# Gathered value rows summed in four column strips instead of two, with seven gather buffers

## The chip, the cores and the metric

The kernel runs on one core of a Trainium2 chip. The metric is the device time of one execution in microseconds (us); runs of the kernel before took 4088.43 to 4096.79 us. Five engines work in parallel, each through its own queue in order: PE (TensorE, matmuls), DVE (VectorE), ACT (ScalarE), POOL (GpSimd, which issues the gathers here) and SP (which issues most other transfers). They wait for each other and for transfers through semaphores.

## The reference, cut to what matters

One layer of a streaming encoder for 1152 tokens (1024 of a prompt, 8 x 16 of running streams) of width 1024: RMS norm, a gated convolution beside an RWKV-7 time mixing, then a retrieval over 16384 single-neuron experts. Only the retrieval's last step is touched by the change:

```python
def block(xt):                                   # 128 tokens
    q = (xt @ wq).reshape(PEER_BLOCK, PEER_HEADS, 2, PEER_HALF)
    ...
    eidx = jnp.take_along_axis(cidx, pos, axis=-1)          # 8 heads x 16 experts a token
    gate = jax.nn.softmax(sc, axis=-1)
    u = jnp.take(U, eidx, axis=0)
    act = jax.nn.gelu(jnp.einsum('thkd,td->thk', u, xt).astype(jnp.float32))
    coef = (gate * act).astype(xt.dtype)
    return jnp.einsum('thk,thkd->td', coef, jnp.take(V, eidx, axis=0))
```

So each token takes 128 rows of U and 128 rows of V, 1024 floats each.

## The kernel before, in words

The nine tiles of 128 tokens go through the time mixing in three groups (`GROUPS`, `base(g)`). The retrieval has two ways. Four tiles (`DENSE`) multiply with all experts (`dense()`): first the gate matrices are made from one-hot products and written to memory (`gates_of`, with `hidden_ahead` beside it), then for each block of 128 experts `hidden` makes the activations (matmuls into `ph`) and `out_half` adds up the outputs (matmuls into `po`). The other five tiles are sparse: they gather only the rows that they need.

- `sparse_u` (L1009) takes a tile's 128 picks k one by one: one indirect DMA, issued by POOL at L1028, fetches the row of U of pick k for all 128 tokens (512 KB into a buffer `gt`), and one DVE instruction multiplies it with the token's input and sums it into column k of `hu`.
- `sparse_v` (L1036) does the same with V, but sums on PE. The coefficients are first transposed, so that partition and pick change places; a gather (L1075) then fetches for one token its 128 rows of V, and a matmul with contraction 128 sums them. The stationary operand is a slice of `cex` of 128 x 32 that is zero but for one column, so the token's sum falls in one of 32 output rows and 32 tokens add up in the same 32 partitions of `pv` (named `sv` in the profile). There are four such column strips of 32. `summed` issues four fp32 matmuls for two tokens, one of strip 2hc+1 and one of strip 2hc for each half of the 1024 columns:

```python
for hf in range(2):
    for c in (1, 0):
        q = 32 * (2 * hc + c)
        mm = P.matmul(pv[q:q + 32, hf * 512:(hf + 1) * 512], cex[:, lo:lo + 32], ...
```

The buffers `gt` are a ring of `NGT` = 6, shared by rows of U, rows of V and a few others; a gather waits until the buffer of the gather six places earlier has been read. `side()` steps through one `sparse_v` and one `sparse_u` at a time, two steps each in turn; a step is one gather. `run` weaves these steps into the main work: before the dense part one step per 900 ns of PE work (`PACE_B`; 1500 ns where only one of the two is there), in it so that they spread evenly over what is left (`until`). PE's queue is in order: a matmul of `sv` whose row has not landed holds up the main work behind it.

The slots `sl` (`NSL` = 27, in `slot()`) hold the time mixing's intermediate tiles. In the first group some gate tiles use `gt` buffers as `room`, since no gather runs then. `hidden` loads one block of `u_t` (512 KB, `ur`), and ACT and DVE split it into two parts for PE.

Of the kernel before, what the change touches and what calls it, by code (L numbers as in the profile page):

```python
# [9 lines left out]
F32 = mybir.dt.float32  # L10
# [20 lines left out]
NPT = 8  # L31
NSL = 27
LAT = 350
SPREAD = (16, 8)
PACE_B = (900, 1500)
EARLY = 40e3
NGT, NGD = 6, 0
AWAY = [4, 5, 6, 7]
# [58 lines left out]
def body(ctx, tc, A):  # L97
# [87 lines left out]
    def f32(ap):  # L185
        return ap.bitcast(F32)
# [130 lines left out]
    def base(g):  # L317
# [18 lines left out]
        if smp:  # L336
            ss = T(bp, [128, KB, 8], F32, "shst", 1)
            nc.sync.dma_start(ss, A["state_shift"])
            S.activation(xh[:, :, n:n + 8], ss, AF.Copy)
            V.tensor_tensor(xl[:, :, n:n + 8], ss, f32(xh[:, :, n:n + 8]), op=OP.subtract)  # L340
# [571 lines left out]
    def route(row, vals, idxs):  # L912
# [62 lines left out]
        yield 6 if row == 0 else 2 * SPREAD[until[0] is not None]  # L975
        gate = T(sp, [128, 8, 16], F32, "gate_d", 1) if row in DENSE else T(sp, [128, 8, 16], F32, "gate", 3)
        V.tensor_tensor(gate, sc, sc[:, :, 0:1].to_broadcast([128, 8, 16]), op=OP.subtract)
# [24 lines left out]

    more = [None, 0]

    def gathered():
# [7 lines left out]
    def sparse_u(row, ei, et, gate):  # L1013
# [12 lines left out]
        for k in range(128):  # L1026
            ug = gathered()
            G.indirect_dma_start(out=ug, out_offset=None, in_=A["peer_u"],  # L1028
                                 in_offset=bass.IndirectOffsetOnAxis(ap=ei[:, k:k + 1], axis=0))
            if due:  # L1030
                dot(*due)
            due = k, ug
            yield
        dot(*due)
        sparse_v_q.append((row, hu, et, gate))

    def sparse_v(row, hu, et, gate):
# [6 lines left out]

        cw = cex[:, :1024].rearrange("p (two c t w) -> p two c t w", two=2, c=2, w=32)
        c4 = ct_.rearrange("p (c b t) -> p c b t", c=4, t=8)

        def fill(n):
            if n < 8:
                V.tensor_copy(cw[:, n % 2, :, :, 31], c4[:, 2 * (n // 4):2 * (n // 4) + 2, n % 4])  # L1050

        def summed(hc, i, vgs):

            prev = mains[1]
            for hf in range(2):
                for c in (1, 0):
                    lo = 32 * (16 * (i // 8 % 2) + 8 * c + i % 8) + 31 - i
                    q = 32 * (2 * hc + c)
                    mm = P.matmul(pv[q:q + 32, hf * 512:(hf + 1) * 512], cex[:, lo:lo + 32],
                                  vgs[c][:, hf * 512:(hf + 1) * 512], start=i == 0, stop=i == 31, side=True)  # L1060
                    behind(mm, prev)
                    prev = mm
            if i % 8 == 0:
                fill(4 * hc + i // 8 + 1)

        fill(0)
        due = None
        for hc, i in ((a, b) for a in range(2) for b in range(32)):
            vgs = []
            for c in range(2):  # L1070
                if c and due:
                    summed(*due)
                t = 64 * hc + 32 * c + i
                vg = gathered()
                G.indirect_dma_start(out=vg, out_offset=None, in_=A["peer_v"],  # L1075
                                     in_offset=bass.IndirectOffsetOnAxis(ap=et[:, t:t + 1], axis=0))
                vgs.append(vg)
                yield
            due = hc, i, vgs
        summed(*due)  # L1080
        live[0] -= 1
# [15 lines left out]
    def dense():  # L1097
# [54 lines left out]
        def hidden(k, g):  # L1152

            raw = T(dp, [128, D], F32, "ur", 2)
            nc.sync.dma_start(raw, A["u_t"][k])
            h = T(dp, [128, D], F32R, "uh", 2)
            S.activation(h, raw, AF.Copy)
            lo = T(dp, [128, D], F32R, "ul", 2)
            V.tensor_tensor(lo, raw, f32(h), op=OP.subtract)
            ps = T(pd, [128, ND], F32, "ph", 2)  # L1160
# [93 lines left out]
    def side():  # L1254

        while True:
# [4 lines left out]
            while two[0] or two[1]:  # L1261
                for i in (0, 0, 1, 1):
                    if two[i] and next(two[i], "end") == "end":
                        two[i] = None
                    elif two[i]:
                        steps[0] += 1
                        yield two.count(None)
# [133 lines left out]
```

## Time and profile before

| | us |
|---|---|
| median of 3 runs (lowest, highest) | 4094.19 (4088.43, 4096.79) |
| the profiled execution, its time | 4107.61 |
| its span, first to last instruction | 4105.8 |
| PE busy, share of the span | 3698.5, 90% |
| DVE, POOL, ACT busy | 2765.4, 1631.3, 1476.1 |
| transfer engines, mean busy share | 75% (queues 47.0, 19.8, 7.9, 0.3) |

The time is read by stages: up to about 1000 us the time mixing with gathers of U only from 580 us on; 1000 to 2200 us the rest of the time mixing, with both kinds of gathers; 2200 to 2600 us the gate matrices; from 2800 to 4050 us the dense products. A busy share says little by itself; what matters in each stage is which engine never waits.

### The profile page before, as it was taken

Reading aid. Unit: us, or ns where it says so; the run is one execution under the profiler, and the core shown is the slowest. Engines: PE = TensorE matmul, PEld = TensorE weight load, DVE = VectorE, ACT = ScalarE, POOL = GpSimd, SP = SyncE. Lnnn points to the kernel's source line nnn. Section 1 sums busy time; section 2 is a strip of 40 time slices with the busy share of each in tenths; the row PEclk is TensorE's granted clock in tenths of the full one; section 3 lists DMA queues with packets and bytes.
Section 4 is the critical chain, followed back from the end, with each engine's and each line's share of the span. In section 5 each row is a group of like instructions: output and inputs, shape, how many; then the busy total and the mean of one; then the engine's idle time right before and its main releaser. Section 6 shows DMA issues by size and latency. Waiting matters only on the chain. (4 is left out here: it accounts for less than half of the span.)

```text
span 4105.8 us, 56088 instructions
## 1 busy us (share of the span) xinstructions
PE 3698.5 (90%) x18870; PEld 2666.7 (65%) x18870; DVE 2765.4 (67%) x7426; ACT 1476.1 (36%) x3383; POOL 1631.3 (40%) x1553
## 2 busy tenths in 40 slices
PE   7999977878897878898869999699999999999998
PEld 6777866666475545455635666488766677766666
DVE  5655799887698786576886555699866666543334
ACT  5455533434332323223235567532322222222222
POOL 0000024434556554555565544455444444333320
PEclk9999988988998988898989999899999999999999
DMA  3223436657998888889888877899999888887774
GB/s 100 74 67 95 159 125 227 224 171 254 342 326 285 319 285 277 284 322 329 306 313 307 312 280 255 306 359 338 333 331 328 282 300 290 292 284 263 251 240 143
DMA packets 415584, 1065.20 MB, mean 259 GB/s; under 512 B 44993, under 2 KB 124993, under 8 KB 413249
## 3 DMA queue, kind: packets, MB, share of 16 engines
q0 software_dynamic: 184464, 671.55, 47.0%
q1 hardware_dynamic: 182880, 271.03, 19.8%
q10 hardware_dynamic: 47952, 119.03, 7.9%
q8 instruction: 150, 2.46, 0.2%
q14 instruction: 138, 1.12, 0.1%
HBM read 1000.55 MB, written 61.28 MB: 259 GB/s over the span
## 5 line engine op out<-in xcount | busy, mean ns | idle before, releaser
L1028 POOL DMA_INDIRECT gt<-peer_u,ei x640 | 786.8, 1229 | 1132.8 <-PE sv L142 467.3
L1075 POOL DMA_INDIRECT gt<-peer_v,et x640 | 679.6, 1062 | 652.9 <-PE sv L142 417.3
L142 PE MATMUL mm<-xT,wh 128*128 128x384 f32 (+1 forms) x2880 | 885.1, 366 | 14.1 <-ACT wh L246 12.9
L159 DVE SCALAR_TENSOR_TENSOR gt<-gt,xn 128x1024 f32<-128x1024 f32 x640 | 772.9, 1220 | 181.3 <-DMA gt<-peer_u,ei 122.6
L142 PE MATMUL sv<-gt,c 128*32 128x512 f32 x2560 | 648.9, 634 | 94.7 <-DMA gt<-peer_v,et 94.6
L142 PE MATMUL po<-vh,ph 128*128 128x512 f32 x2048 | 652.7, 392 | 0.0
L142 PEld LDWEIGHTS mm<-xT,wh 128*128 128x128 f32 x2880 | 554.7, 197 | 91.9 <-issue 45.4
L142 PE MATMUL mm<-xT,wl 128*128 128x384 f32 (+1 forms) x1440 | 509.5, 354 | 42.1 <-DVE wl L159 36.4
L142 PEld LDWEIGHTS po<-vh,ph 128*128 128x128 f32 x2048 | 383.2, 188 | 105.1 <-issue 23.5
L142 PE MATMUL ph<-xth,uh 128*128 128x512 f32 x1024 | 412.6, 403 | 31.9 <-ACT ge L1168 31.9
L142 PE MATMUL ph<-xth,ul 128*128 128x512 f32 x1024 | 405.9, 396 | 0.0
L142 PE MATMUL ph<-xtl,uh 128*128 128x512 f32 x1024 | 404.5, 395 | 0.0
L142 PEld LDWEIGHTS sv<-gt,c 128*32 128x32 f32 x2560 | 126.7, 113 | 423.7 <-issue 299.3
L142 PE MATMUL po<-vl,ph 128*128 128x512 f32 x1024 | 401.2, 392 | 0.0
L246 ACT ACTIVATE wh<-raw 128x512 fp32r<-128x512 f32 x432 | 268.6, 628 | 352.0 <-PE mm L142 196.8
L159 DVE TENSOR_TENSOR wl<-raw,wh 128x512 fp32r<-128x512 f32 x432 | 295.1, 686 | 99.5 <-ACT wh L246 85.4
L142 PEld LDWEIGHTS mm<-xT,wl 128*128 128x128 f32 x1440 | 285.2, 198 | 71.4 <-DVE wl L159 47.3
L1195 ACT ACTIVATE vh<-vr 128x512 fp32r<-128x512 f32 x256 | 159.7, 627 | 370.2 <-PE po L142 265.6
L159 DVE TENSOR_TENSOR ge<-ge,cc 128x512 f32<-128x512 f32 x128 | 87.8, 689 | 298.9 <-ACT ge L1168 262.7
L159 DVE TENSOR_SCALAR o<-iota,dt 128x128 f32<-128x128 f32 x640 | 177.4, 347 | 146.8 <-PE po L142 146.4
L1168 ACT ACTIVATE ge<-ph 128x512 f32<-128x512 f32 x128 | 76.4, 598 | 554.6 <-PE ph L142 545.9
L142 PEld LDWEIGHTS ph<-xth,uh 128*128 128x128 f32 x1024 | 193.1, 189 | 116.6 <-issue 41.9
(247 smaller groups left out, 5287.1 us busy)
## 6 DMA issues: line engine op xcount, KB each, us to landing
ur<-u_t SPq DMA_DIRECT2D x128, 512.0 KB
vr<-peer_v ACTq DMA_DIRECT2D x256, 256.0 KB
raw<-w_in SPq DMA_DIRECT2D x240, 256.0 KB
c<-ct ACTq DMA_DIRECT2D x16, 2048.0 KB
cc<-c SPq DMA_DIRECT2D x32, 1024.0 KB
raw<-peer_wq SPq DMA_DIRECT2D x96, 256.0 KB
raw<-w_pab SPq DMA_DIRECT2D x48, 256.0 KB
raw<-w_o SPq DMA_DIRECT2D x48, 256.0 KB
```

The source lines that it names most:

```text
L142: ins = nc.tensor.matmul(out, lhsT, rhs, **kw)
L159: self.last = getattr(nc.vector, name)(*a, **kw)
L246: S.activation(h, part, AF.Copy)
L1028: G.indirect_dma_start(out=ug, out_offset=None, in_=A["peer_u"], in_offset=bass.IndirectOffsetOnAxis(ap=ei[:, k:k + 1], axis=0))
L1075: G.indirect_dma_start(out=vg, out_offset=None, in_=A["peer_v"], in_offset=bass.IndirectOffsetOnAxis(ap=et[:, t:t + 1], axis=0))
L1168: S.activation(g, ps, AF.Gelu_apprx_tanh)
L1195: S.activation(h, raw, AF.Copy)
```

## The change

`sparse_v` now takes four tokens at a time, one of each strip, and issues eight matmuls for them in the order of strips 3, 2, 1, 0 for each half. The sum of four tokens is issued after the third gather of U that follows them when both kinds run (`both`), else after two more gathers of V. `side()` takes four gathers of V, then four of U. The ring `gt` has seven buffers. To make room for it: `NSL` falls to 25, two small tiles share others' buffers (`shst`, `gate_d`), and `hidden` loads `u_t` in two halves of 128 x 512, each split by its own ACT and DVE instruction.

```diff
-NSL = 27
+NSL = 25
...
-NGT, NGD = 6, 0
+NGT, NGD = 7, 0
...
-            ss = T(bp, [128, KB, 8], F32, "shst", 1)
+            ss = T(bp, [128, KB, 8], F32, "bc", 3)
...
-        gate = T(sp, [128, 8, 16], F32, "gate_d", 1) if row in DENSE else T(sp, [128, 8, 16], F32, "gate", 3)
+        gate = T(sp, [128, 8, 16], F32, "d1", 1) if row in DENSE else T(sp, [128, 8, 16], F32, "gate", 3)
...
-        cw = cex[:, :1024].rearrange("p (two c t w) -> p two c t w", two=2, c=2, w=32)
-        c4 = ct_.rearrange("p (c b t) -> p c b t", c=4, t=8)
+        cw = cex[:, :1024].rearrange("p (two c t w) -> p two c t w", two=2, c=4, w=32)
+        c4 = ct_.rearrange("p (c b t) -> p c b t", c=4, t=4)
...
-                for c in (1, 0):
-                    lo = 32 * (16 * (i // 8 % 2) + 8 * c + i % 8) + 31 - i
-                    q = 32 * (2 * hc + c)
+                for c in (3, 2, 1, 0):
+                    lo = 32 * (16 * (i // 4 % 2) + 4 * c + i % 4) + 31 - i
+                    q = 32 * c
...
-        for hc, i in ((a, b) for a in range(2) for b in range(32)):
+        for i in range(32):
             vgs = []
-            for c in range(2):
-                if c and due:
+            for c in range(4):
+                if c == 2 and due:
                     summed(*due)
-                t = 64 * hc + 32 * c + i
+                    due = None
+                t = 32 * c + i
                 vg = gathered()
                 G.indirect_dma_start(out=vg, out_offset=None, in_=A["peer_v"],
                                      in_offset=bass.IndirectOffsetOnAxis(ap=et[:, t:t + 1], axis=0))
                 vgs.append(vg)
-                yield
-            due = hc, i, vgs
-        summed(*due)
+                yield True
+            due = i, vgs
+            yield False
+            if both[0]:
+                summed(*due)
+                due = None
+                yield False
...
-            raw = T(dp, [128, D], F32, "ur", 2)
-            nc.sync.dma_start(raw, A["u_t"][k])
             h = T(dp, [128, D], F32R, "uh", 2)
-            S.activation(h, raw, AF.Copy)
             lo = T(dp, [128, D], F32R, "ul", 2)
-            V.tensor_tensor(lo, raw, f32(h), op=OP.subtract)
+            for c in range(2):
+                cs = slice(512 * c, 512 * c + 512)
+                raw = T(dp, [128, 512], F32, "ur", 2)
+                nc.sync.dma_start(raw, A["u_t"][k][:, cs])
+                S.activation(h[:, cs], raw, AF.Copy)
+                V.tensor_tensor(lo[:, cs], raw, f32(h[:, cs]), op=OP.subtract)
...
-                for i in (0, 0, 1, 1):
-                    if two[i] and next(two[i], "end") == "end":
+                for i in (0, 0, 0, 0, 0, 1, 1, 1, 0, 1):
+                    both[0] = two[1] is not None
+                    if two[i] is None:
+                        continue
+                    got = next(two[i], None)
+                    if got is None:
                         two[i] = None
-                    elif two[i]:
+                    elif got:
                         steps[0] += 1
                         yield two.count(None)
```

PE's queue in the gate stage, kernel before; `sv` is the strip accumulator, `gt` a gathered row, `c` the coefficients. Two sums follow each other with other matmuls between them:

```order
L142 MATMUL sv_4405_19284<-gt_4856_20946,c_17_108 32x512 [waits DMASW6_49]
L142 MATMUL sv_4405_19284<-gt_4850_20918,c_17_108 32x512 [waits DMASW5_49]
L142 MATMUL sv_4405_19284<-gt_4856_20946,c_17_108 32x512
L142 MATMUL sv_4405_19284<-gt_4850_20918,c_17_108 32x512
...
L142 MATMUL sv_4405_19284<-gt_4879_21034,c_17_108 32x512 [waits DMASW0_49]
L142 MATMUL sv_4405_19284<-gt_4878_21011,c_17_108 32x512 [waits DMASW7_49]
L142 MATMUL sv_4405_19284<-gt_4879_21034,c_17_108 32x512
L142 MATMUL sv_4405_19284<-gt_4878_21011,c_17_108 32x512
```

The same place now:

```order
L142 MATMUL sv_4404_19283<-gt_4890_21077,c_17_108 32x512 [waits DMASW0_49]
L142 MATMUL sv_4404_19283<-gt_4889_21058,c_17_108 32x512 [waits DMASW7_49]
L142 MATMUL sv_4404_19283<-gt_4867_20985,c_17_108 32x512 [waits DMASW6_49]
L142 MATMUL sv_4404_19283<-gt_4860_20957,c_17_108 32x512 [waits DMASW5_49]
L142 MATMUL sv_4404_19283<-gt_4890_21077,c_17_108 32x512
L142 MATMUL sv_4404_19283<-gt_4889_21058,c_17_108 32x512
L142 MATMUL sv_4404_19283<-gt_4867_20985,c_17_108 32x512
L142 MATMUL sv_4404_19283<-gt_4860_20957,c_17_108 32x512
```

The matmuls are as many as before, but eight stand together where four did, half as many times, and the first four wait for four landed rows.

POOL's queue in the dense stage where both kinds of gathers run, kernel before (the first semaphores named are of earlier transfers into the same buffer):

```order
L1028 DMA gt_6686_27715<-peer_u,ei_5531_23300 128x1024 [waits DMASW6_49,DMASW3_49,PE_49]
L1028 DMA gt_6687_27718<-peer_u,ei_5531_23300 128x1024 [waits DMASW5_49,DMASW4_49,PE_49]
L1075 DMA gt_6688_27721<-peer_v,et_4830_20856 128x1024 [waits DVE_49]
L1075 DMA gt_6689_27727<-peer_v,et_4830_20856 128x1024 [waits DVE_49]
L1028 DMA gt_6690_27729<-peer_u,ei_5531_23300 128x1024 [waits DMASW7_49,DMASW2_49,PE_49]
L1028 DMA gt_6698_27770<-peer_u,ei_5531_23300 128x1024 [waits DMASW1_49,DMASW0_49,PE_49]
```

And now:

```order
L1029 DMA gt_6760_28025<-peer_u,ei_5560_23411 128x1024 [waits DMASW0_49,DVE_49]
L1077 DMA gt_6761_28028<-peer_v,et_4840_20899 128x1024 [waits DMASW4_49,DMASW1_49,PE_49]
L1077 DMA gt_6762_28030<-peer_v,et_4840_20899 128x1024 [waits DMASW3_49,DMASW2_49,PE_49]
L1077 DMA gt_6787_28154<-peer_v,et_4840_20899 128x1024 [waits PE_49]
L1077 DMA gt_6788_28156<-peer_v,et_4840_20899 128x1024 [waits PE_49]
L1029 DMA gt_6789_28158<-peer_u,ei_5560_23411 128x1024 [waits DMASW5_49,DVE_49]
L1029 DMA gt_6790_28161<-peer_u,ei_5560_23411 128x1024 [waits DMASW6_49,DVE_49]
L1029 DMA gt_6791_28164<-peer_u,ei_5560_23411 128x1024 [waits DMASW7_49,DVE_49]
```

Gathers now come four and four, and the ones that wait for PE (for a sum to free a buffer) are mostly those of V instead of those of U.

## Rows read from the trace of the kernel before

**Rows 1.** Busy time of each engine by stage; granted clock, transfer share, GB/s last.
```profile
core 0: us, PE busy (x) PEld busy (x) DVE busy (x) ACT busy (x) POOL busy (x), PEclk, DMA share, GB/s
...
2800.00:3000.00 200.00, 200.00 (x877) 157.01 (x876) 171.15 (x277) 59.50 (x92) 91.93 (x77) 1.00 0.95 336
...
1000.00:2200.00 1200.00, 1010.20 (x5329) 666.68 (x5328) 912.20 (x2921) 394.14 (x962) 654.46 (x587) 0.91 0.88 310
2200.00:2600.00 400.00, 386.64 (x2038) 255.93 (x2037) 219.86 (x715) 256.00 (x598) 197.97 (x222) 0.99 0.79 284
2600.00:2800.00 200.00, 166.62 (x731) 137.78 (x730) 165.12 (x271) 59.80 (x95) 96.84 (x74) 0.91 0.95 332
2800.00:4050.00 1250.00, 1247.87 (x5380) 857.58 (x5379) 709.37 (x1104) 308.39 (x476) 475.74 (x436) 1.00 0.85 291
3000.00:3600.00 600.00, 600.00 (x2585) 419.14 (x2584) 370.48 (x576) 150.83 (x230) 250.35 (x225) 1.00 0.88 304
```

**Rows 2.** The same stretches, PE instructions of tile `sv` alone: busy, records.
```profile
1000.00:2200.00 1200.00, 298.27 (x1075) 0.91 0.88 310
2200.00:2600.00 400.00, 111.26 (x464) 0.99 0.79 284
...
2800.00:4050.00 1250.00, 240.71 (x1026) 1.00 0.85 291
3000.00:3600.00 600.00, 104.50 (x440) 1.00 0.88 304
```

**Rows 3.** The page's costliest groups, the sums; then PE's waits for gathers, 1000 to 2200.
```profile
L142 PE MATMUL sv<-gt,c 128*32 128x512 f32 x2560 | 648.9, 634 | 94.7 <-DMA gt<-peer_v,et 94.6
...
  DMA gt<-peer_v,et: 87.9, 31
```

**Rows 4.** Timeline of PE around one sum of the dense stage: start, us, instruction.
```profile
3424.07 0.39 PE L142 MATMUL ph<-xth,ul 128*128 128x512 f32 x1
3424.30 0.39 PE L142 MATMUL ph<-xtl,uh 128*128 128x512 f32 x1
3424.61 1.91 PE L142 MATMUL sv<-gt,c 128*32 128x512 f32 x8
3426.46 0.50 PE L142 MATMUL ph<-xth,uh 128*128 128x512 f32 x1
3426.79 0.39 PE L142 MATMUL ph<-xth,ul 128*128 128x512 f32 x1
```

**Rows 5.** Another sum in windows of 0.2 us: records of `sv` alive in each.
```profile
3399.50:3399.70 0.20, 0.15 (x2) 1.00 1.18 420
3399.70:3399.90 0.20, 0.20 (x2) 1.00 0.99 348
3399.90:3400.10 0.20, 0.20 (x4) 1.00 1.01 297
```

**Rows 6.** Timeline of PE: one fp32 matmul of 64 columns; its records, min/median/max ns.
```profile
154.25 0.38 PE L142 MATMUL rk<-c,ar 128*64 128x128 f32 x2
154.56 0.44 PE L142 MATMUL mm<-xT,wh 128*128 128x384 f32 x1
...
L142 PE MATMUL rk<-c,ar x64: 272/275/421, 1438.2 to 1761.8; 128*64 128x128 f32 x64
```

**Rows 7.** Gathers of V and a sum that waited; gathers of U (min/median/max ns); tile gt.
```profile
1290.66 0.95 POOL L1075 DMA_INDIRECT gt<-peer_v,et  x1 [0.30 <-DVE cand L159]
1291.92 0.95 POOL L1075 DMA_INDIRECT gt<-peer_v,et  x1 [0.30 <-DVE r L159]
...
1299.49 1.91 PE L142 MATMUL sv<-gt,c 128*32 128x512 f32 x8 [1.48 <-DMA gt<-peer_v,et]
...
L1028 POOL DMA_INDIRECT gt<-peer_u,ei x640: 935/1086/3142, 585.0 to 3614.4; - x160
...
1600.00:1800.00 200.00, 53.40 (x190) 10.11 (x192) 55.08 (x90) 0.00 (x0) 100.93 (x92) 0.87 0.83 285
```

**Rows 8.** Splitting of `u_t` and of tiles half as wide; matmuls of `hidden`, 2800 to 4050.
```profile
L1157 ACT ACTIVATE uh<-ur x128: 1039/1052/1077, 2088.8 to 4025.5; 128x1024 fp32r<-128x1024 f32 x128
...
L159 DVE TENSOR_TENSOR ul<-ur,uh x128: 1166/1225/1303, 2091.9 to 4026.6; 128x1024 fp32r<-128x1024 f32 x128
...
L246 ACT ACTIVATE wh<-raw 128x512 fp32r<-128x512 f32 x432 | 268.6, 628 | 352.0 <-PE mm L142 196.8
L159 DVE TENSOR_TENSOR wl<-raw,wh 128x512 fp32r<-128x512 f32 x432 | 295.1, 686 | 99.5 <-ACT wh L246 85.4
...
L142 PE MATMUL ph<-xth,ul 128*128 128x512 f32 x613 | 241.5, 394 | 0.0
```

**Rows 9.** Waits of SP's transfer queue, 1000 to 1400 and 1400 to 1800: us, times, longest.
```profile
SPq L256 <- DVE wl L159: 144.9, 52, 16.3
...
SPq L836 <- PE rk L142: 16.1, 1, 16.1
```

More of the change, by code (lines that the diff above doesn't have):

```diff
@@ L1003, in body @@
     more = [None, 0]
+    both = [False]
     def gathered():
@@ L1043, in sparse_v, with summed @@
         V.tensor_copy(ct_, pv[:, 0:128])
-        cw = cex[:, :1024].rearrange("p (two c t w) -> p two c t w", two=2, c=2, w=32)
-        c4 = ct_.rearrange("p (c b t) -> p c b t", c=4, t=8)
+        cw = cex[:, :1024].rearrange("p (two c t w) -> p two c t w", two=2, c=4, w=32)
+        c4 = ct_.rearrange("p (c b t) -> p c b t", c=4, t=4)
         def fill(n):
             if n < 8:
-                V.tensor_copy(cw[:, n % 2, :, :, 31], c4[:, 2 * (n // 4):2 * (n // 4) + 2, n % 4])
-        def summed(hc, i, vgs):
+                V.tensor_copy(cw[:, n % 2, :, :, 31], c4[:, :, n])
+        def summed(i, vgs):
             prev = mains[1]
             for hf in range(2):
-                for c in (1, 0):
-                    lo = 32 * (16 * (i // 8 % 2) + 8 * c + i % 8) + 31 - i
-                    q = 32 * (2 * hc + c)
+                for c in (3, 2, 1, 0):
+                    lo = 32 * (16 * (i // 4 % 2) + 4 * c + i % 4) + 31 - i
+                    q = 32 * c
                     mm = P.matmul(pv[q:q + 32, hf * 512:(hf + 1) * 512], cex[:, lo:lo + 32],
@@ L1062, in summed @@
                     prev = mm
-            if i % 8 == 0:
-                fill(4 * hc + i // 8 + 1)
+            if i % 4 == 0:
+                fill(i // 4 + 1)
         fill(0)
         due = None
-        for hc, i in ((a, b) for a in range(2) for b in range(32)):
+        for i in range(32):
             vgs = []
-            for c in range(2):
-                if c and due:
+            for c in range(4):
+                if c == 2 and due:
                     summed(*due)
-                t = 64 * hc + 32 * c + i
+                    due = None
+                t = 32 * c + i
                 vg = gathered()
@@ L1077, in sparse_v @@
                 vgs.append(vg)
-                yield
-            due = hc, i, vgs
-        summed(*due)
+                yield True
+            due = i, vgs
[4 more added lines that the diff above has]
+                yield False
+        if due:
+            summed(*due)
         live[0] -= 1
```

## The prediction

> **What bounds the kernel now.** I read the busy time by stage first, because the shares of the whole span mix four stages [rows 1]. Look at PE and at the transfer share. From 2800 to 4050 us PE is busy 1247.87 of 1250 us at granted clock 1.00: in this dense stage every microsecond of PE work is one of run time, and nothing else need be asked. In the gate stage, 2200 to 2600, PE is busy 386.64 of 400, nearly the same. In the time mixing with both gathers, 1000 to 2200, PE is busy 1010.20 of 1200, the granted clock is 0.91 (a mean over its two levels, 1.2 and 2.4 GHz), DVE is busy 912.20 and the transfers have a share of 0.88: no engine is full, but two resources are near it. From 2600 to 2800 no rows of V are summed, so the change's main edit does not touch it. Before 1000 us there are no sums either.
>
> Then I read what the sums cost PE: tile sv is 298.27 us in the time mixing, 111.26 in the gate stage, 240.71 in the dense stage [rows 2], 648.9 in all, with 94.6 us more in which PE stood idle until a gathered row had landed [rows 3], 87.9 of them between 1000 and 2200. So the sums are some 16% of the run, and a third of that lies where PE is the only bound.
>
> **What four strips do to a sum.** The program has 1280 matmuls of sv (5 tiles x 128 rows x 2 halves), the trace 2560 records: an fp32 matmul leaves two. The question is whether two records that run together are two strips or the two parts of one matmul. In a sum of two rows two records live at any time, four where one pair hands over to the next, some 0.43 us after the first [rows 5]. A lone fp32 matmul of 64 columns tells which: its two records last 0.38 us together, where a single one lasts 0.27, and the next instruction starts 0.31 us later [rows 6]; its two parts go one after the other (128 moving columns four times over at 2.4 GHz are 0.213 us). So the records that start together in a sum belong to different strips, and two strips do run side by side: four matmuls of 4 x 512 / 2.4 GHz = 0.853 us each would take 3.41 us in a row, and the sum's successor starts 1.85 us after it [rows 4].
>
> A whole sum costs PE more than its 1.85 us. Before it, the next matmul would have started 0.23 us after 3424.30 but the sum starts at 3424.61 (0.08 lost); behind it, the second matmul comes 0.33 us after the first where 0.23 is usual (0.10 lost). That is 2.03 us for two rows. If four strips run side by side as two do, eight matmuls for four rows take the same 2.03 us, and half of the sums are gone:
> - dense stage: 1024 records / 8 = 128 sums, 64 fewer, 64 x 2.03 = 130 us of PE time;
> - gate stage: 464 / 8 = 58 sums, 29 fewer, 59 us;
> - time mixing: 1075 / 8 = 134 sums, which cost 298.27 / 134 = 2.23 us each at the lower clock, with the 0.18 around them 2.4; 67 fewer, 160 us.
>
> The trace has no sum with four strips. Its time lies between 1.85 us (strips fully side by side) and 3.7 us (two at a time, nothing gained). I take the first: nothing in the rows distinguishes strips 2 and 3 from 0 and 1, and both pairs run so today.
>
> A rule speaks somewhat against it. Two strips here gain 3.41 / 1.71 = 2.0x (two pairs of 0.853 us instead of four in a row). The Trainium skill (TensorE: Matmul & The Clock Gate, Part 3) gives 2.38x for three column tiles, not 3x; no run here shows three. By the page's ratio four strips would give some 3.2x, an estimate from that page: 2.15 us for the eight matmuls, and some 50 us less saved over 160 sums.
>
> **How much of it reaches the end.**
> *Dense stage, 130 us of PE.* PE never waits, so all of it counts unless transfers become late. Their share of 0.85 over 1250 us becomes 0.95 over 1120. Between 2800 and 3000 the trace has 0.95 with PE busy 200 of 200 us, so that rate can be carried. From 3000 to 3600 the 440 records make 55 sums, 27.5 fewer, 56 us: 0.88 x 600 / 544 = 0.97, just above what the trace has shown. I take off 15 us: **115**.
> *Gate stage, 59 us.* The share goes from 0.79 to 0.93; ACT, busy 256 of 400 us, would be 75% busy. The one-hot tiles that PE waits for come from ACT, DVE and POOL, so some wait grows: **45**.
> *Time mixing, 160 us.* Here the transfers decide: 0.88 x 1200 = 1056, which at 0.95 needs 1112 us, so at most 88 us can be gained, and DVE would stand at 912.20 / 1112 = 82%. The clock, already 0.91 where PE has pauses, will not rise with less PE work. I take 85 before the costs below.
>
> **What the rest of the change costs.**
> *Gathers.* The ring of six with two and two had this lead: a gather of V can go once the sum two sums before its own is done, eight gathers earlier. The ring of seven with four and four lets the last of four rows go once the previous sum is done, again eight gathers earlier. In the time mixing eight gathers take about 17 us (92 in 200 us); the last of the four has four others ahead of it at 1.1 us and about 0.3 us between them, near 7 us, and lands within about 7.6 us of its start [rows 7]: 14.6 of 17. The lead holds, with little to spare, as it did; and there are half as many places to stall. I leave the 88 us of stalls as they are: 0, with bounds of a gain of 60 and a loss of 88. In the dense stage gathers are 2.7 us apart (225 in 600 us), and the lead is 21 us.
> *POOL's queue.* Behind a gather that waits stand the norms' powers, the memsets and the one-hots; they wait now for a sum of four. Their readers have other matmuls on PE ahead of them, as before: 0; uncovered, a few us for each power, some tens of us in all.
> *u_t in halves.* ACT pays 2 x 628 instead of 1052 ns, DVE 2 x 686 instead of 1225 [rows 8], 128 times: 26 and 19 us, on engines busy 308.39 and 709.37 of 1250 us: 0. SP issues 128 more transfers. The lookahead falls from two blocks to one; a block is used every 16 us (613 records of one kind / 8 = 77 blocks in 1250 us, also [rows 8]), loading and splitting take under 10. If that cover failed PE would wait a few us per block, up to 100 us in all.
> *Slots.* Two fewer of 27. SP's queue already waits for slots and buffers to be read, 144.9 us behind the weights' splitting and up to 16.1 us for one transfer into a slot, with weights queued behind it [rows 9]. In the first group one more gate tile lies in gt, which gives both back. In the other two groups a few slots are reused sooner: 10 us, bounds 0 and 30.
>
> So the time mixing gives 85 - 10 = 75, and the sum is 115 + 45 + 75 = **235 us**. The profiled execution took 4107.61 us, 13.4 above the median of 4094.19; from the median the forecast is 4094 - 235 = **3859**, say 3860 us.
>
> **The rivals.**
> *Two strips at a time.* If the array takes only two strips together, a sum of four takes 3.7 us, PE time stays, and only half of the switches (160 x 0.18 = 29 us) and some stalls are saved, less the slots: about 4060, between 4010 and 4110. For it: no row shows four. Against it: the pairs now used are both neighbours and both run together.
> *Partly side by side.* Each further strip costs something, as if the four moving operands shared a way in: 2.65 us instead of 1.85, halfway to nothing gained by the bounds above. That is 160 x 0.8 = 128 us less saved on PE, about half of it felt: 3930. For it: no row; the page's ratio above lies at this case's near end. Against it: the pairs' handover of 0.43 us shows no lag for two.
> *Transfers become the bound.* The same bytes in less time: if 0.92 is the most that mixed traffic carries, the time mixing gives 52 (1056 / 0.92 = 1148), the dense stage 95 (0.85 x 1250 / 0.92 = 1155), the gate stage 30, and late rows take back 60: 4094 - 117 = 3977.
> *Slower: the ring locks step.* Four buffers are held until the last of four rows has landed, and only three rows of U can be under way meanwhile. If each of the 160 sums then holds PE up by t us, the gain of 235 is gone at t = 1.5; at t = 2, 320 us are lost and the run takes 4094 + 85 = 4180. For it: the lead in the time mixing is 2 to 3 us only, and a quicker kernel makes it shorter. Against it: in the dense stage the lead is 21 us for 14 needed.
>
> **How the numbers follow.** Forecast 0.68 (3790 to 3950); transfers bound 0.08; partly side by side 0.08; two at a time 0.10; lock step 0.06. The range reaches up over partly side by side and the transfers' case to 4010, and down to 3770, where the stalls go and the time mixing gains all that transfers at a share of 1 would allow. A difference under 0.2% (8 us) can't be told from none. Faster: 0.68 + 0.08 + 0.08 + 0.06 of the two at a time = 0.90; same 0.03; slower 0.07.
>
> **What would show it.** Right: sums of sixteen records that last 1.9 us, four records alive at once; sv busy near 330 us in all; a dense stage of about 1130 us with PE still full; transfer shares of 0.93 to 0.96 in the time mixing. Wrong: sums of 3.6 us (strips), or PE's waits for gt<-peer_v well above 95 us (ring), or PE below 95% in the dense stage with waits for ur, vr or gt (transfers).

## The result and the profile after

The changed kernel takes **3949.31 us** (median; 3941.97 to 3953.4) beside 4095.49 us of the kernel before on the same chip: a ratio of 0.9642, 95% interval 0.962 to 0.9665. That is 146 us less, where the prediction expected 235: the time of 3949 lies inside the range of 3770 to 4010, and 89 us above the forecast of 3860. It is at the upper edge of the band from 3790 to 3950 that the prediction gave its own case, and between the times of two of its rivals (3930 and 3977). So the time alone does not tell which of them came true; the trace has to.

The profiled execution took 3941.97 us with a span of 3940.2. The page's heaviest group, to be read against the first line of [rows 3]: line, engine, operation, tiles, shape, count | busy us, mean ns | idle us before it, and what ended most of it.

```profile
L142 PE MATMUL sv<-gt,c 128*32 128x512 f32 x2560 | 338.1, 650 | 146.4 <-DMA gt<-peer_v,et 142.2
```

The number of records is the same and a record lasts as long, yet PE is busy with them for 338.1 us instead of 648.9. PE's wait for gathered rows has grown from 94.6 to 142.2.

One sum of the dense stage, in PE's timeline (the answer to [rows 4]), and the records of `sv` alive in windows of 0.2 us from its start (the answer to [rows 5]):

```profile
3313.48 1.92 PE L142 MATMUL sv<-gt,c 128*32 128x512 f32 x16 [1.89 <-DMA gt<-peer_v,et]
3315.33 0.50 PE L142 MATMUL ph<-xth,uh 128*128 128x512 f32 x1
```

```profile
3313.40:3313.60 0.20, 0.12 (x4) 1.00 1.20 448
3313.60:3313.80 0.20, 0.20 (x4) 1.00 0.95 348
3313.80:3314.00 0.20, 0.20 (x8) 1.00 1.00 351
```

Sixteen records, eight matmuls, fill the 1.85 us that eight records filled before. Four records run at a time, and eight at the handover, where there were two and four.

For the loss of the other 89 us, the run has to be cut into its stages by landmarks that both kernels have: the first sum, the first matmul into `ph` (the gate stage begins), the first matmul of `po` from `vh` (the dense stage begins), the end. Busy time by stage, of the kernel before and then of the changed one; the columns are those of [rows 1]:

```profile
1040.40:2123.80 1083.40, 904.97 (x4800) 589.44 (x4800) 809.68 (x2610) 324.57 (x812) 594.30 (x528) 0.91 0.88 309
2123.80:2644.90 521.10, 472.38 (x2468) 316.23 (x2467) 306.11 (x995) 320.71 (x738) 256.30 (x279) 0.96 0.81 292
2644.90:4105.80 1460.90, 1447.44 (x6259) 1022.52 (x6257) 882.14 (x1383) 372.68 (x584) 561.18 (x504) 1.00 0.84 289
```

```profile
1031.40:2091.90 1060.50, 801.28 (x4799) 588.42 (x4799) 802.91 (x2601) 329.36 (x822) 581.63 (x514) 0.86 0.87 309
2091.90:2566.70 474.80, 416.98 (x2499) 309.62 (x2497) 308.01 (x1034) 320.09 (x773) 257.71 (x285) 0.96 0.90 328
2566.70:3940.20 1373.50, 1331.65 (x6251) 1003.27 (x6251) 897.54 (x1490) 382.42 (x672) 586.37 (x512) 0.99 0.88 310
```

| stage | before, us | after, us | gained | predicted | PE busy | PE idle |
|---|---|---|---|---|---|---|
| up to the first sum | 1040.4 | 1031.4 | 9 | none | | |
| time mixing with sums | 1083.4 | 1060.5 | 23 | 75 | -104 | 178 to 259 |
| gate stage | 521.1 | 474.8 | 46 | 45 | -55 | 49 to 58 |
| dense stage to the end | 1460.9 | 1373.5 | 87 | 115 | -116 | 13 to 42 |

These add up to 165.6 us, the difference of the two profiled executions; that of the medians is 146. So the table accounts for 69 of the 89 us, and the other 20 are the distance of the two profiled executions from their medians. The predicted figures were for stretches cut at 1000, 2200, 2600 and 2800 us; cut by the landmarks, the time mixing of the kernel before has 1001 records of sums instead of 1075, and the gate stage 537 instead of 464.

PE does less work in every stage, as predicted. In the time mixing most of that came back as idle time: of 104 us less work, 81 are lost. Who held PE up there, as waits by engine, line and tile (us, times, longest; before, then after):

```profile
PE sv L142 <- DMA gt<-peer_v,et: 85.9, 30, 7.8
PE mm L142 <- DVE wl L159: 23.7, 17, 3.3
```

```profile
PE sv L142 <- DMA gt<-peer_v,et: 110.0, 26, 14.3
PE mm L142 <- DVE wl L159: 51.2, 34, 4.7
PE rk L147 <- DVE mt L159: 16.7, 4, 8.8
```

Half as many sums wait nearly as often and longer, up to 14.3 us. These waits are 24 of the 81 us; waits for weights that DVE splits (wl) are 27.5 more, and the rest is spread over smaller ones. POOL in its turn waited for sums to free buffers, before and after:

```profile
POOL gt L1028 <- PE sv L142: 259.5, 97, 8.0
```

```profile
POOL gt L1029 <- PE sv L142: 213.1, 42, 8.9
```

One turn of the gathers in the changed kernel, from the timeline of POOL (start, us, instruction, and in brackets the idle time before it with what ended it) and of PE:

```profile
1383.76 2.00 POOL L1029 DMA_INDIRECT gt<-peer_u,ei  x1 [8.17 <-PE sv L142]
...
1390.85 1.86 POOL L1077 DMA_INDIRECT gt<-peer_v,et  x1 [0.31 <-DVE wl L159]
1393.01 1.06 POOL L1029 DMA_INDIRECT gt<-peer_u,ei  x1 [0.30 <-DVE a L159]
1394.38 0.95 POOL L1029 DMA_INDIRECT gt<-peer_u,ei  x1 [0.30 <-DVE bc L159]
1395.63 0.94 POOL L1029 DMA_INDIRECT gt<-peer_u,ei  x1 [0.30 <-DVE bc L159]
1400.38 1.65 POOL L1029 DMA_INDIRECT gt<-peer_u,ei  x1 [3.81 <-PE sv L142]
```

```profile
1395.18 0.34 PE L142 MATMUL mm<-xT,wh 128*128 128x384 f32 x1
1398.20 1.93 PE L142 MATMUL sv<-gt,c 128*32 128x512 f32 x16 [2.68 <-DMA gt<-peer_v,et]
```

The last of the four rows of V is issued at 1390.85 (the three before it are left out here). Three gathers of U follow; then POOL stands, since the eighth needs a buffer that the sum holds. PE's sum stands, 2.68 us, until that last row has landed at 1398.20, 7.35 us after its issue began. The sum ends at 1400.1, and the next turn begins. Everything in this circle waits for the next thing in it. From one restart of POOL to the next, 1383.76 to 1400.38, it takes 16.62 us: 7.09 until the gather of the last row begins, 7.35 until that row has landed, 1.93 for the sum and 0.25 until POOL goes on. Not every turn closes like this one: POOL waited for a sum 42 times and a sum for rows 26 times, in some 61 turns.

### The profile page after: what moved, and what is told of

Same layout as the page of the kernel before. It is cut to its first block, busy times and chain, and to the rows that moved or that the text cites. A ratio compares the mean times of both kernels' runs of the same rounds, so it can differ in the third digit from the quotient of the medians.

```text
span 3940.2 us, 56486 instructions
## 1 busy us (share of the span) xinstructions
PE 3416.1 (87%) x18870; PEld 2633.5 (67%) x18870; DVE 2769.8 (70%) x7554; ACT 1486.2 (38%) x3511; POOL 1644.5 (42%) x1553
## 5 line engine op out<-in xcount | busy, mean ns | idle before, releaser
L1029 POOL DMA_INDIRECT gt<-peer_u,ei x640 | 764.5, 1194 | 1160.4 <-DVE gt L159 442.5
L1077 POOL DMA_INDIRECT gt<-peer_v,et x640 | 713.3, 1115 | 484.1 <-PE sv L142 283.4
L142 PE MATMUL sv<-gt,c 128*32 128x512 f32 x2560 | 338.1, 650 | 146.4 <-DMA gt<-peer_v,et 142.2
L142 PEld LDWEIGHTS sv<-gt,c 128*32 128x32 f32 x2560 | 70.5, 115 | 307.4 <-DMA gt<-peer_v,et 162.2
L142 PEld LDWEIGHTS po<-vl,ph 128*128 128x128 f32 x1024 | 192.9, 188 | 55.7 <-DVE vl L159 15.4
L142 PEld LDWEIGHTS ph<-xth,ul 128*128 128x128 f32 x1024 | 193.4, 189 | 54.1 <-issue 6.7
```

The lines of the kernel that those rows point to most:

```text
L142: ins = nc.tensor.matmul(out, lhsT, rhs, **kw)
```

## The experiments

Four theories, as the expectations name them. **A**: the sums' PE time is the whole matter, and the other edits cost nothing. **B**: four rows at a time in a ring of seven hold the gathers up, 60 to 80 us. **C**: the order in which the kernel's own scheduler (it places instructions by a simulated timeline) lays the program out decides, not the edits. **D**, formed after the first eight runs and a sharper B: the circle above sets the time mixing. Differences between kernels that ran apart are taken through the kernel before in the same set (4087.91, 4107.85 and 4094.5 us).

### Less work for PE without fours, and with them

```diff
 # b_half: the kernel before; a_half: the changed kernel
-            for hf in range(2):
+            for hf in range(1):
 # and the closing sum reads the one half twice
-            V.tensor_tensor(y[:, hf * 512:(hf + 1) * 512], pv[:, hf * 512:(hf + 1) * 512],
+            V.tensor_tensor(y[:, hf * 512:(hf + 1) * 512], pv[:, 0:512],
```

> The kernel before, with only the first half of the columns summed: two matmuls for two rows instead of four, same gathers, same ring of six, no other edit. It leaves out the second half of the value sums. Each of the 320 sums loses 0.85 us of PE, 273 us in all, nearly what the change took from PE (310 us of sv). Theory A (what PE loses in sums is worth its size in the dense and gate stages, and little in the time mixing, where PE then waits longer for rows and weights; the other edits cost nothing): about the change's own time less the 29 us of switches that stay, 3975 us, 3955 to 3995. Theory B (the other edits, four rows at a time in a ring of seven above all, hide 60 to 80 us of what PE saved): 3880 to 3910.

Measured: 3886.23 us, ratio 0.9505 (0.9486 to 0.9523).

> The changed kernel with only the first half of the columns summed: four matmuls for four rows instead of eight, everything else the same. It leaves out the second half of the value sums. Each of 160 sums loses 0.85 us: 54 us in the dense stage, 30 in the gate stage, 52 in the time mixing. Theory A: the dense stage gives some 45, the gate stage 20, the time mixing 5 to 10: 3875 us, 3860 to 3895. If the time mixing still follows PE (theory B): 3835 to 3855.

Measured: 3858.48 us, ratio 0.9438 (0.942 to 0.9455). b_half takes as much work off PE as the change does (sv 367.24 us busy over the three stages), and gains 202 us where the change gains 146. In the stage in question, b_half's time mixing and, under it, the `sv` records in it:

```profile
1041.40:2056.90 1015.50, 812.41 (x4290) 580.19 (x4289) 799.86 (x2600) 323.76 (x817) 582.97 (x516) 0.86 0.91 323
...
1041.40:2056.90 1015.50, 154.32 (x489) 0.86 0.91 323
```

It lasts 1015.5 us, 45 less than the changed kernel's, with 154.32 us of sums against 146.18. So the stage could use the PE time, and something that came with the change took it back (b_half has none of its other edits). A falls by b_half, with one reserve: another order of the same work moves this kernel by as much (a_pairs, below). The time of a_half lies between the ranges of both theories; with the sums of the change halved once more, it gets 1042.1 us there, still 27 above b_half, with 83.18 us of sums: what sets the stage is not PE's work on sums any more.

### The strips, and the buffers

```diff
 # a_pairs: the changed kernel; two strips' both halves, then the other two's
-            for hf in range(2):
-                for c in (3, 2, 1, 0):
+            for cs in ((3, 2), (1, 0)):
+                for hf, c in ((0, cs[0]), (0, cs[1]), (1, cs[0]), (1, cs[1])):
```

> The changed kernel with the eight matmuls of a sum in another order, strips 3 and 2 for both halves and then strips 1 and 0, so that two strips run at a time and not four. All gathers, buffers and waits as in the changed kernel. A sum should take 3.6 us instead of 1.85. Theory A (four strips at once are the whole gain, the rest costs nothing): 4095 less the 20 to 29 us of switches that are gone, 4070 us, 4055 to 4090. Theory B (the rest costs 60 to 80): 4135 to 4160. If the order of strips did not matter: 3950.

Measured: 4039.28 us, ratio 0.9883 (0.9866 to 0.9901). A sum of it in PE's timeline:

```profile
3379.68 1.94 PE L142 MATMUL sv<-gt,c 128*32 128x512 f32 x16
3381.55 0.50 PE L142 MATMUL po<-vh,ph 128*128 128x512 f32 x1
```

The edit didn't do what it was made for: written as 3, 2, 3, 2, 1, 0, 1, 0 the eight matmuls still last 1.87 us, so the four strips still ran together. The sum costs the same, and the kernel is some 98 us slower than the changed one. Its time mixing lasts 1139.4 us; it holds 510 gathers instead of 482, at 2.23 us each instead of 2.20, so most of those 79 us are gathers that came earlier. Its dense stage is 27 us longer with 10 gathers fewer. An edit that changes nothing in the work can thus move this kernel by 2%, presumably through the order that the scheduler makes of it; why the dense stage is longer stays open. A difference in the time of one variant is to be read with that in mind.

```diff
 # b_room7: the kernel before, with the change's edits of memory alone
-NSL = 27
+NSL = 25
-NGT, NGD = 6, 0
+NGT, NGD = 7, 0
 # and ss in "bc", gate in "d1", u_t in halves, as in the change
```

> The kernel before with all edits that make room and the seventh buffer (25 slots, two shared tiles, u_t in halves, ring of seven), but rows still summed two at a time and gathered two and two. Theory A: 4095, 4080 to 4105: the slots and the halves cost nothing and the seventh buffer has little to give. Theory B1 (the slots and halves cost what is missing): 4130 to 4175. Rival: a seventh buffer ends the 95 us of waits for rows of V: 4020 to 4060.

Measured: 4099.32 us, ratio 1.0026 (1.0014 to 1.0039): 11 us slower. The memory edits cost that much even with a ring of seven and two rows to a sum, whose waits for rows of V fall to 50.8 us in the time mixing (85.9 before). The stage is hardly shorter for it, 1081.4 instead of 1083.4 us, with 515 gathers instead of 496; the rival, by which the end of these waits gives 4020 to 4060, falls. The dense stage has 24 us of idle PE instead of 13.

### The overlap alone

```diff
 # a_fwd: the changed kernel, strips in ascending order
-                for c in (3, 2, 1, 0):
+                for c in (0, 1, 2, 3):
```

> The changed kernel with the strips of a sum issued 0, 1, 2, 3 instead of 3, 2, 1, 0. For the chip the work is the same; the kernel's scheduler, which orders each engine's instructions by its own reckoning, lays them out in another order (1750 of DVE's 6088 rows stand elsewhere). The strips in pairs did the same sums in 1.87 us and still took 90 us more. Theory C (the layout's order decides how much of the saved PE time comes through, in the time mixing above all): 3960 to 4040, off the changed kernel by more than 10 us, with the difference in the stretch from the first sum to the gate stage. Theory A or B (the order is nothing): 3940 to 3958.

Measured: 4128.83 us, ratio 1.0053 (1.0036 to 1.007). It was to be an idle edit and was not one: the time lies far outside the ranges of all the theories. PE's timeline, and the page's group:

```profile
1400.55 1.05 PE L142 MATMUL sv<-gt,c 128*32 128x512 f32 x2
1403.07 1.90 PE L142 MATMUL sv<-gt,c 128*32 128x512 f32 x10
...
L142 PE MATMUL sv<-gt,c 128*32 128x512 f32 x2560 | 643.8, 622 | 79.4 <-DMA gt<-peer_v,et 75.4
```

The scheduler now puts other matmuls between the strips: single ones of two records that last 1.05 us alone, and a rest of five. Sums are busy 643.8 us, as before the change. What is left is the change without most of its overlap: 21 us slower than the kernel before, 11 of which b_room7 has as well. The way from the changed kernel to this one is 167 us, more than the 98 of a_pairs, and goes with 306 us more of sums on PE. So the gain is the overlap's, and it hangs on the strips' matmuls standing in a row. A likely reason for the difference, argued and not tested: in the order 3, 2, 1, 0 the first matmul waits for the row that was gathered last, and the other three rows have then landed.

### The scheduler

```diff
-    with tile.TileContext(nc, schedule_with_timeline_sim=True) as tc:
+    with tile.TileContext(nc, schedule_with_timeline_sim=False) as tc:
```

> The changed kernel, its instructions laid out by the plain scheduler (schedule_with_timeline_sim=False), which doesn't reckon with times. Nothing else is altered. To be read against the kernel before laid out the same way. Theory C: the gain between the two is nearer to the 235 us of the forecast than to 146, 190 to 250. Theory B (four rows at a time cost 50 us by themselves): 130 to 165.

> The kernel before, laid out by the plain scheduler. Its own time is open, 4050 to 4200; what counts is the distance to the changed kernel laid out in the same way: 190 to 250 us by theory C, 130 to 165 by theory B.

Measured: 4169.45 us, ratio 1.0152 (1.0135 to 1.0169), for the changed kernel, 4280.47 us, 1.0423 (1.0405 to 1.044), for the one before, both laid out without the simulated timeline. The gap of 111 us is smaller than the 146 with it, and below the ranges of both theories (190 to 250, 130 to 165). So this layout did not keep the gain down: C falls as the cause, though layout moves single variants. The time mixing with fours is here longer than with pairs, 1176.8 against 1120.4 us, although its sums keep PE busy for 184.74 us instead of 285.20. That fours cost something in this stage is thus seen without the simulated timeline as well.

### The bytes

```diff
 # a_narrow: the changed kernel, half of each row of V
-                G.indirect_dma_start(out=vg, out_offset=None, in_=A["peer_v"],
+                G.indirect_dma_start(out=vg[:, 0:512], out_offset=None,
+                                     in_=A["peer_v"].rearrange("n (h d) -> (n h) d", h=2),
```

> The changed kernel with each gather of V fetching 512 columns instead of 1024, and both matmuls of a row reading these 512: 168 MB of 1065 less to move, the same count of gathers and matmuls. It leaves out half of the value rows' data. If transfers hold back the time mixing (the third rival of the prediction): its waits for rows of V fall from 110 to under 50 us and the stretch from the first sum to the gate stage from 1060 to about 990; the whole 3850 to 3890. If the waits are a matter of order and of the ring alone: 3930 to 3950.

Measured: 3966.28 us, ratio 0.9667 (0.9642 to 0.9692). With 168 MB less to carry, a transfer share of 0.77 in the time mixing instead of 0.87, and 100.5 us of waits for rows of V, the kernel is no quicker, and slower than either theory had it. Its time mixing is even longer, 1108.1 us, with 514 gathers instead of 482. The bytes of the rows of V were thus not the bound, and with half rows of V PE waits nearly as long as with whole ones.

### The ring

Two kernels in which only the ring differs. Both fetch half rows of U and V, so that two rows fit one buffer.

```diff
 # a_r7 (TWO = False) and a_r14 (TWO = True), in gathered(); who is 0 for U, 1 for V
+        if not TWO:
+            return T(sp, [128, D], F32, "gt", NGT)[:, 0:512]
+        if kept[who] is None:
+            kept[who] = T(sp, [128, D], F32, "gt", NGT)
+            return kept[who][:, 0:512]
+        got, kept[who] = kept[who][:, 512:1024], None
+        return got
```

> The changed kernel, with gathers of U and of V that fetch only half of each row (512 columns, into the first half of a buffer); the products with U run over 512 columns, both halves of a sum read the same 512. The ring still holds seven rows. It is the control for the next kernel. Theory D (lock step of the ring): in the time mixing a gather waits for a sum, the sum waits for the last of its four rows, and only three gathers of U are issued between that row and the waiting gather, whatever the rows weigh; the waits for rows of V stay near 100 us there, the stage near 1040 to 1100 us. Rival (the waits come from the load of the transfers or of DVE, which is lighter here by half of its products): waits below 50 us, the stage below 1010 us.

Measured: 3787.29 us, ratio 0.9259 (0.9231 to 0.9286).

> The kernel with half rows, as the one before, but two rows share a buffer: two of V from one sum, or two successive ones of U. The seven buffers then hold fourteen rows; instructions, bytes and sums are the same. Theory D: a sum's rows can be under way while the previous sum still waits, so the waits for rows of V in the time mixing fall below 50 us and the stage is 40 to 70 us shorter than with one row to a buffer; the whole kernel 50 to 100 us quicker than that one. Rival (the ring does not matter, the waits are the price of issuing on POOL or of the landing): the same within 15 us, waits within 20 us.

Measured: 3682.15 us, ratio 0.8993 (0.8969 to 0.9017): 105 us quicker than with one row to a buffer. The time mixing of a_r7 and the `sv` records in it, and PE's wait for rows there; then the same of a_r14:

```profile
980.70:1990.60 1009.90, 797.74 (x4864) 580.42 (x4864) 691.59 (x2646) 336.12 (x833) 563.61 (x547) 0.87 0.68 210
...
980.70:1990.60 1009.90, 156.81 (x1042) 0.87 0.68 210
...
PE sv L143 <- DMA gt<-peer_v,et: 70.7, 33, 10.0
```

```profile
986.20:1907.20 921.00, 771.60 (x4858) 576.28 (x4859) 686.00 (x2641) 334.04 (x832) 556.33 (x547) 0.89 0.73 230
...
986.20:1907.20 921.00, 138.69 (x1042) 0.89 0.73 230
...
PE sv L143 <- DMA gt<-peer_v,et: 5.6, 3, 3.3
```

Both have 1042 records of sums and 514 gathers in that stage; with the longer ring it is 89 us shorter. PE's wait for rows of V falls from 70.7 to 5.6 us, its idle time from 212 to 149, and its busy time from 798 to 772, since PE paused less and was granted 0.89 instead of 0.87 of its clock. The gate stage is alike (449.2 and 447.4). This is D's picture, and more than the 40 to 70 us that it expected; the wait that all but ends, and not the time alone, sets it off from a mere other layout. D was wrong on a_r7, though: waits of 70.7 instead of near 100, and a stage of 1009.9 instead of 1040 to 1100 us. And a_r7 is 162 us quicker than the changed kernel with the same ring. With both kinds of rows halved a row of V lands in 4.4 us (median) instead of 7.0, which shortens the same circle; products half as long on DVE shorten the run as well, and these two were not told apart.

```diff
 # a_ring6: the changed kernel
-NGT, NGD = 7, 0
+NGT, NGD = 6, 0
-                for i in (0, 0, 0, 0, 0, 1, 1, 1, 0, 1):
+                for i in (0, 0, 0, 0, 0, 1, 1, 0, 1, 1):
```

> The changed kernel with six buffers instead of seven; the sum is emitted after two gathers of U instead of three, all else is kept. Theory D: the lead falls by one gather, so each of some 61 sums of the time mixing is held up by 1.1 to 1.7 us more: that stage 60 to 100 us longer than 1060, the kernel at 4010 to 4060 us. Rival (the seventh buffer gives nothing, as the lead is longer than a landing): within 15 us of the changed kernel's 3949.

Measured: 4073.49 us, ratio 0.996 (0.9932 to 0.9988). One buffer fewer costs 124 us, nearly the whole gain. It is a little more than D said, but in another place, so D's forecast for the stage failed: the time mixing lasts 1068.4 us, only 8 more, with 447 gathers instead of 482. A gather takes 2.39 us there instead of 2.20. The gate stage is 23 us longer; the gathers left over come in the dense stage, 83 us longer, whose idle PE goes from 42 to 96 us (67.5 of it for rows of V).

```diff
 # a_pace1050: the changed kernel
-PACE_B = (900, 1500)
+PACE_B = (1050, 1500)
```

> The changed kernel with its pace of gathers in the stages with both kinds at one gather for every 1050 ns of planned PE work instead of 900: fewer gathers in the time mixing and the gate stage, more in the dense stage, where they have a longer lead. Theory D: the time mixing is set by its number of turns of eight gathers (some 61 of 16.6 us); with some 9 turns fewer it gets 40 to 100 us shorter, and the dense stage longer by 9 sums of 2 us: 3870 to 3930 us in all. Rival (the time mixing is bound by PE, by the clock or by other work): the sums only move, 2.2 us here for 2.0 us there, and the kernel is within 15 us of 3949, or slower where gathers are late at the end.

Measured: 3944.33 us, ratio 0.9637 (0.9613 to 0.9661): the same as the changed kernel. The time mixing is 49 us shorter, as D has it (443 gathers instead of 482), the gate stage 3 us longer, and the dense stage 36 us longer, since it has 1378 records of sums instead of 1026. For the total the rival was right: the sums only moved. This way of moving gathers does not get round the circle.

## Why the prediction was right, and where it was off

**Strips: right.** The sum of sixteen records takes the 1.85 us that was put into the working, sv is busy 338.1 us (near 330 was said). Each fp32 matmul of 512 columns being 0.853 us, eight in a row would take 6.8 us: four strips give 3.7 times by the 1.85 us, where two gave 1.8 (4.0 and 2.0 without what lies at the ends of a sum, as the prediction counted). The rivals of two at a time and of partly side by side fall with it. The Trainium skill's ratio for three column tiles (TensorE: Matmul & The Clock Gate, Part 3: 2.38x) gave an estimate of 2.15 us for this sum; the trace does not agree, and the measurement decides.

**Gate stage: the number right, in part by luck.** It gave 46 us for 45 predicted. But the stage as cut here has 537 records of sums, for which the prediction's own rate gives some 68 us of PE work (estimate: 34 sums of 2.03 us) where 55 went. And two waits of PE there moved against each other: the one for rows of V grew, and a single one for ACT shrank, which the prediction had not. Before, then after:

```profile
PE ph L142 <- ACT ge L1168: 31.9, 1, 31.9
PE sv L142 <- DMA gt<-peer_v,et: 6.6, 3, 2.4
```

```profile
PE sv L142 <- DMA gt<-peer_v,et: 23.4, 5, 15.2
PE ph L142 <- ACT ge L1178: 11.0, 1, 11.0
```

**Dense stage: PE's part right, the end off by 28.** Sums there fall from 240.71 to 123.72 us, 117 for the 130 that the working had with what lies around a sum, and PE's busy time by 116. But the prediction let only 15 us go for late transfers, and PE is idle 42 us instead of 13. PE's waits there in the changed kernel:

```profile
PE po L142 <- DVE vl L159: 9.2, 8, 2.0
PE sv L142 <- DMA gt<-peer_v,et: 8.8, 10, 1.9
PE po L142 <- ACT vh L1205: 7.8, 6, 2.6
PE ph L142 <- ACT uh L1168: 4.5, 4, 1.5
```

Weights whose halves are split late (vl, vh, uh: 21.5 us) and rows of V. b_room7 has 11 us of the 28 without any four. The share of the transfers is 0.88, not 0.95. What makes the blocks of `peer_v` late was not tried.

**Time mixing: the term that was mis-sized.** It gave 23 us where 75 stood, 32 with the 9 us by which it begins earlier. b_half, which takes as much PE work away and has none of the other edits, gave 68 in this stage, so the 85 put down before the costs were not far off. The PE work fell as said: sums by 133 us (279.15 to 146.18), 29 of which came back since PE with more pauses got 0.86 instead of 0.91 of its clock (3,800 other records: 626 us before, 655 after). What failed is the step on gathers: "The lead holds, with little to spare, as it did", taken as 0. It set 14.6 us (7 until the last row's gather begins, 7.6 until it lands) against the 17 of eight gathers. Both terms came out so in the turn shown above, 7.09 and 7.35. (Four gathers at 1.4 us make 5.6, not 7, but two of these took some 2 us each.) The sum itself, 1.93 us, and the 0.25 until POOL goes on belong to the same turn, and were left out: 16.62 of 17, next to nothing to spare. Nor was it "as it did": the kernel before has three gathers ahead of the last row's instead of four, so 1.4 to 1.8 us more to spare (an estimate from the same turn). The same lead can be counted from the other side, from the last row of a sum to the first gather that must wait for that sum. With N buffers and R rows to a sum N - R gathers stand between. The changed kernel has three for a landing of 7.0 us (the last figure of this line of its DMA issues), the kernel before had four.

```profile
gt<-peer_v,et POOLq DMA_INDIRECT x640, 7.0
```

Three gathers take 3 x 0.95 and their gaps of 0.30, some 4 us. In order of the lead, the time mixing's length by the gathers of both kinds in it, and PE's wait for rows of V there:

| kernel | buffers, rows to a sum | gathers free to go | us for each gather | PE's wait, us |
|---|---|---|---|---|
| a_ring6 | 6, 4 | 2 | 1068.4 / 447 = 2.39 | 99.2 |
| after | 7, 4 | 3 | 1060.5 / 482 = 2.20 | 110.0 |
| a_half | 7, 4 | 3 | 1042.1 / 499 = 2.09 | 110.2 |
| a_pairs | 7, 4 | 3 | 1139.4 / 510 = 2.23 | 147.3 |
| a_fwd | 7, 4 | 3 | 1128.3 / 490 = 2.30 | 73.0 |
| a_narrow, half rows of V | 7, 4 | 3 | 1108.1 / 514 = 2.16 | 100.5 |
| a_pace1050 | 7, 4 | 3 | 1011.3 / 443 = 2.28 | 75.5 |
| before | 6, 2 | 4 | 1083.4 / 496 = 2.18 | 85.9 |
| b_half | 6, 2 | 4 | 1015.5 / 484 = 2.10 | 94.5 |
| b_room7 | 7, 2 | 5 | 1081.4 / 515 = 2.10 | 50.8 |
| a_r7, half rows | 7, 4 | 3 | 1009.9 / 514 = 1.96 | 70.7 |
| a_r14, half rows | 14, 4 | 10 | 921.0 / 514 = 1.79 | 5.6 |

With three gathers free the whole rows of U give 2.09 to 2.30 us, nearly as wide a spread as between two gathers free and five. So the table does not show that the lead alone sets this time; a_r7 and a_r14, alike but for the ring, show that it counts. b_half puts all that came with the change other than PE's work at 45 us in this stage, of which the prediction had 10 (the slots); the ring of fourteen half rows gives 89. How much of the 45 is the lead, how much the layout, stays open. A ring of eight whole rows does not fit beside the other buffers and was not tried.

**The rival that came true in part** is the ring that locks step. One of the prediction's signs of being wrong came up for it: waits for rows of V of 142.2 us, where "well above 95" was the sign. In the time mixing PE is idle for 81 us more, of which b_half has 25 without fours; the other 56, over 61 sums, are 0.9 us a sum. That is below the 1.5 from which it would have eaten the gain, and only 24 us of it are waits for the rows themselves. It was confined to this stage in the main (8.8 us of such waits in the dense one), where, as the prediction said against it, gathers are rarer: 506 in 1373.5 us, one in 2.7. In a_ring6 it shows there too. The transfers as the bound: a share of 0.87 in the time mixing, where 0.93 to 0.96 was forecast, and a_narrow speak against it.

**The other costs.** Slots, halves of `u_t` and shared tiles were put at 10 us, with bounds of 0 and 30; b_room7 measured 11, with a longer ring's gain in it. PE's wait for `uh` in the dense stage, 4.5 us, is what is seen there of the shorter lookahead.

## What to carry to other kernels

Where a step frees several buffers at once, add up one whole turn: the issues until its last input, the landing, the step itself and the restart. Then hold the sum against the time in which the stage needs a turn. Or count the issues that may go between its last input and the first one that needs a buffer back, and hold their time against the landing: by that count a step that takes two rows more wants two buffers more, not one. PE time saved in a stage whose turn is set by such a circle comes back as waiting, and here some of it once more as a lower clock (0.91 to 0.86). A gain on the engine that is full nearly all the time came through for the most part, 87 of 116 us in the dense stage and 46 of 55 in the gate stage, against 23 of 104 in the time mixing.

## What the runs showed of the hardware

Four 32-column strips of fp32 matmuls ran side by side, 1.85 us for eight of 512 columns, as long as four took in two strips. They did so also when the program had them as 3, 2, 3, 2, 1, 0, 1, 0; one pair after the other would have needed 3.4 us, and 2.6 if each matmul had begun only after the one ahead of it in that order had begun (three times 0.853, an estimate); they took 1.87. Strips 1 and 0 were thus under way before the second matmuls of strips 3 and 2, which stand ahead of theirs in the program, had begun. Half the bytes of the rows of V alone hardly changed how long PE waits for them: 100.5 us, 110.0 with whole ones. With rows of U and V both halved a row of V landed in 4.4 us instead of 7.0.
